# Seven block products in place of eight for three pairs of gate units, and ring buffers in another order

## The chip, the cores and the metric

The kernel runs on one core of a Trainium2 chip. The metric is the time of one execution on the device, in microseconds (us); lower is better. Before the change the median of 3 runs is 960.73 us (960.54 to 960.83). The core's engines are named as the profile names them: PE (TensorE, matrix products), DVE (VectorE), ACT (ScalarE), POOL (GpSimd) and SP (SyncE, which here issues nearly all DMAs).

## The reference, cut to what matters

One encoder layer on 512 tokens of 1024 columns: three token mixers side by side, a gated sum of them, an output projection, a norm, and a mixture of 16 experts of which each picks 64 tokens.

```python
z = jnp.einsum('bsd,df->bsf', x, w_in[l])
q_na, k_na, v_na, q_g, k_g, v_g, q_m, gate_logits = jnp.split(z, _split_points(), axis=-1)
...
branches = jnp.stack([y_na, y_gqa, y_mem], axis=2)                 # 3 mixers, 512 wide each
proj = jnp.einsum('bsgk,gkd->bsgd', branches, w_branch[l])
gates = jax.nn.sigmoid(gate_logits + b_gate[l]).reshape(B, S, N_BRANCH, D)
merged = jnp.sum(gates * proj, axis=2)
mix = jnp.einsum('bsd,de->bse', merged, w_out[l])
x = layer_norm(DN_ALPHA * x + mix, ln1_g[l], ln1_b[l])
ffn = expert_choice_ffn(x, w_router[l], w_gate_up[l], w_down[l])
x = layer_norm(DN_ALPHA * x + ffn, ln2_g[l], ln2_b[l])
```

The change concerns `gate_logits` of the last mixer that is computed, the neighbourhood attention (NA, branch 0): a product of the 512 tokens with a 1024 x 1024 block of `w_in`.

## The kernel before

**Weights as units.** All weights of the mixers, `w_in`, `w_branch` and `w_out`, come as 74 units of 512 KB (`wu`), tiles of 128 partitions x 1024 fp32 values. Class `Stream` brings them in program order: `_dma` has SP load the next unit into one half of the tile `raw_twin`, `_split` makes two tiles of it, a high part (ACT casts to fp32r, L100) and a low part (DVE subtracts the high part from the value, L101). `prefetch` keeps splits ahead of use and up to two loads ahead of the splits.

**A gate unit.** A unit of `w_in` holds 128 output columns for all 8 blocks of 128 inputs. `t_unit` multiplies it with the tokens, which lie transposed and split as `xh` and `xl`: for each of the 8 blocks three matmuls of 128 x 512, high x high, high x low and low x high (L284 to L286), 24 in all, summed in one PSUM buffer. A gate unit ends with a tanh on ACT (L505), which reads PSUM and writes the tile `sg`. The gates of NA are units 54 to 61, eight in a row (`g_na_gates`); then come units 62 to 65 (`w_branch` of NA, products `pr`) and 66 to 73 (`w_out`, products `wo`).

**Order.** The kernel stands under a manual schedule: each engine executes its instructions in program order. `run(gen, every)` drives a generator of PE work and, at each of its yields, steps the attention and takes one item from the list `bg`. While the gates run, `bg` holds three small steps of the router: `router_scale` (four DVE operations), `router_sums` (one small matmul into the PSUM tile `wps`) and `router_centre` (two DVE operations that read `wps`). PSUM has buffers of four tags: `mm` 3, `S` 2, `T` 2, `Y` 1; gates, `pr` and `wps` take `mm` in turn.

**Expert weights.** Behind the units come the experts' weights, 2 MB or 1 MB a block, loaded by SP into homes in SBUF in the order of `RING`; a home is a tile that an earlier stage must have left. `Ring.load` issues a block, and SP waits there until the home is free. The first loads are put behind loads of units by the table `after`: `_dma` calls `after[i]` behind unit i. What else fits comes behind the output projection's units with `ring.upto`, and then a block each time one is used up.

```python
    def gate_piece(g, j, dst):
        u, = ws.take()
        ws.prefetch()
        acc = PB("mm", f"gate{g}{j}")
        t_unit(acc, u, xh, xl)
        return lambda: nc.scalar.activation(dst, acc, AF.Tanh, bias=bg_t[:, g * 8 + j:g * 8 + j + 1], scale=0.5)
```

Of the kernel before, what the change touches and what calls it, by code (L numbers as in the profile page):

```python
# [18 lines left out]
P = 128  # L19
D = 1024  # L20
S = 512
KD = 8
# [50 lines left out]
def layer_kernel(ctx: ExitStack, tc: tile.TileContext, xt, xn, first0, wu, bgate, rpb, gains, wrt,  # L73
                 lnp, lnt, wx, csn, nmask, tri, iota, out, dbg=None):
    nc = tc.nc
# [12 lines left out]
    def R(tag, shape, name, dt=F32, bufs=None):  # L88
        return rp.tile(shape, dt, name=name, tag=tag, bufs=bufs)
# [3 lines left out]
    def PB(tag, name, shape=(P, 512)):  # L93
        return ps.tile(list(shape), F32, name=name, tag=tag, bufs=PS_BUFS[tag])
# [4 lines left out]
    def hi_lo(hi, lo, src):  # L99
        nc.scalar.copy(hi, src)  # L100
        nc.vector.tensor_tensor(lo, src, hi.bitcast(F32), op=ALU.subtract)  # L101
# [40 lines left out]
    def home(i):  # L142
        if NV + 2 <= i < NV + 4:
            if not wide_v:
                wide_v.append(R("Q3", [P, 4, 1024], "whl_v", F32R))
            j = 2 * (i - NV - 2)
            return wide_v[0][:, j], wide_v[0][:, j + 1]
        i = (i - 2 * (i >= NV + 4) - NV) % 3
        return los[:, 3] if i == 2 else R("hi", [P, 1024], f"whi{i}", F32R, bufs=2), los[:, i]


    class Stream:
        AHEAD_DMA = 2

        def __init__(self):
            self.nd = 0
            self.ns = 0
            self.used = 0
            self.raw = {}
            self.hl = {}  # L160

        def _dma(self):
            i = self.nd
            if 2 <= i < 10:
                if i in (2, 6):
# [4 lines left out]
            nc.sync.dma_start(t, wu[i])  # L170
            self.raw[i] = t
            self.nd += 1
            for f in after.pop(i, ()):
                f()
# [28 lines left out]
    after = {}  # L203
    ws = Stream()
# [18 lines left out]
    xh = R("G0", [P, KD, S], "xh", F32R)  # L223
    xl = R("G1", [P, KD, S], "xl", F32R)
# [34 lines left out]
    bg_t = consts[:, 480:504]  # L259
# [74 lines left out]
    ST = {}  # L334
# [50 lines left out]
    bg = []  # L385
# [128 lines left out]
    def g_branch(g, first, pre=None):  # L514
        if first:
            ST["macc"] = R("M", [P, KD, S], "macc")
        macc = ST["macc"]
        for jp in range(4):
            th = []
            for jj in range(2):  # L520
                t = R("t", [P, S], f"th{g}{jp}{jj}", bufs=2)
                th.append(t)
                ev = gate_piece(g, 2 * jp + jj, t)
                yield
                ev()
# [12 lines left out]
            if pre:  # L538
                yield from pre(jp)

    def g_na_qk(hp):
# [4 lines left out]
        for i in range(2):  # L546
# [5 lines left out]
            for h in range(2):  # L552
# [8 lines left out]
                else:  # L561
# [3 lines left out]
                    for o in (hb, lb):  # L565
                        nc.vector.tensor_tensor(klo[o:o + 64, h], src, k[o:o + 64].bitcast(F32), op=ALU.subtract)

    def g_na_gates():
        sg = R("Q4", [P, KD, S], "sg")
        ST["sg"] = sg  # L570
        for j in range(8):
            ev = gate_piece(0, j, sg[:, j])
            yield
            ev()


    def recip_norm(pt, sm, heads):
# [102 lines left out]
    def na_bias(hp):  # L680
        bf = R("bf", [P, 2, 8, 48], f"bf{hp}")
        for bq in range(2):
            for c in range(8):
                p0 = bq * 64 + c
                nc.sync.dma_start(bf[p0:p0 + 57:8], bass.AP(
                    tensor=rpb.tensor, offset=rpb.offset + 2 * hp * 8 * 63 + 15 - 8 * bq - c,
                    ap=[[64 * 63, 8], [63, 16], [1, 48]]))
        if hp % 2 == 0:
            bm = R("Q4", [P, 2, 3, 256], f"bm{hp}")
        else:  # L690
            bm = ST["b01"][:, 2:4].rearrange("p a n -> p (a n)")[:, :1536].rearrange("p (h t n) -> p h t n", h=2, t=3)
        for ty in range(3):
            for h in range(2):
                nc.gpsimd.tensor_tensor(
                    bm[:, h, ty].rearrange("p (b r c) -> p r b c", b=4, r=8),
                    bf[:, h, :, 16 - 8 * ty:48 - 8 * ty].rearrange("p r (b c) -> p r b c", b=4),
                    mask_t[:, ty, None, :].to_broadcast([P, 8, 32]).rearrange("p r (b c) -> p r b c", b=4),
                    op=ALU.add)
        ST[f"bm{hp}"] = bm
# [69 lines left out]
    class Attn:  # L769
# [4 lines left out]
        def add(self, us):  # L774
            self.units += us
# [144 lines left out]
    wsum = wtmp[:, 4][:, :2 * NEXP].rearrange("p (a e) -> p a e", a=2)  # L920
# [75 lines left out]
    def load_x1(h):  # L996
        nc.sync.dma_start(X1[:, 2 * h:2 * h + 2], xn[:, 2 * h:2 * h + 2])
# [1 line left out]
    def x1(m):  # L999
        return X1[:, m]  # L1000

    for i, f in enumerate((lambda: load_x1(0), lambda: load_x1(1), lambda: ring.more(5), load_tri, lambda: ring.more(6))):
        after[N_UNITS - 5 + i] = [f]
    run(g_na_proj())
    top = cp.tile([48, 64], F32, name="top")
# [117 lines left out]
    for kp in range(4):  # L1123
        u, = ws.take()
# [759 lines left out]
```

## Time and profile before

| | us |
|---|---|
| median of 3 runs | 960.73 |
| the profiled execution, its own time | 960.27 |
| its span in the trace | 958.5 |
| PE busy | 942.4 (98%) |
| weight loads of PE (beside matmuls) | 608.5 (63%) |
| DVE busy | 451.1 (47%) |
| ACT busy | 277.3 (29%) |
| POOL busy | 97.4 (10%) |

DMA moves 251.18 MB, a mean of 262 GB/s over the span. "Busy" of PE includes time in which its pipelined matmuls wait for operands that stream in, so 98% doesn't say that PE is the limit everywhere. The page cuts the span into 40 slices of 24 us; one row there shows the rate of DMA in each slice. Slices 0 to 15 are mixers with little DMA, slices 21 to 38 are the experts; the gates of NA fall into slices 15 to 17. A row of a timeline or of a group reads: engine, line, operation, output tile <- input tiles, partitions x elements.

### The profile page before, as it was taken

The numbers are of one execution on the slowest core, as the hardware profiler recorded it, in microseconds if no ns is written. First come the engines' busy times: TensorE is split into PE (matmuls) and PEld (weight loads), VectorE is DVE, ScalarE is ACT, GpSimd is POOL, SyncE is SP. The second block draws the span as 40 slices with busy tenths as digits, with TensorE's granted clock in tenths as the row PEclk, the third lists the DMA queues.
The fourth block names the chain that finished last, engine by engine and source line by source line (L and its number), as shares of the span: only waits on it lengthen the run. The fifth ranks groups of instructions, "written<-read, shape, count | busy, mean of one in ns | idle before, by whom it ended". The sixth has DMA issues, their size and how long they took to land.

```text
span 958.5 us, 12982 instructions
## 1 busy us (share of the span) xinstructions
PE 942.4 (98%) x5262; PEld 608.5 (63%) x5262; DVE 451.1 (47%) x855; ACT 277.3 (29%) x545; POOL 97.4 (10%) x112
## 2 busy tenths in 40 slices
PE   9999999999999999999999999999999999999997
PEld 9899878888888888888886333433334333533345
DVE  6347668764376567237464121653222313231426
ACT  6334453543344454233232111100011000100123
POOL 0102303000122231000023004000000000000004
PEclk9999999999999999999999999999999999999999
DMA  9321211211433322566929999999999999999992
GB/s 363 114 67 67 66 67 44 67 48 64 116 85 110 103 83 66 206 247 262 377 78 381 428 428 424 426 431 430 429 431 430 431 430 431 429 431 429 431 420 111
DMA packets 40807, 251.18 MB, mean 262 GB/s; under 512 B 13198, under 2 KB 13582, under 8 KB 25516
## 3 DMA queue, kind: packets, MB, share of 16 engines
q1 hardware_dynamic: 40604, 250.10, 64.8%
q8 instruction: 41, 0.67, 0.3%
q10 hardware_dynamic: 144, 0.26, 0.1%
q14 instruction: 18, 0.15, 0.0%
HBM read 247.46 MB, written 2.10 MB: 260 GB/s over the span
## 4 chain that ended last, share of the span: by engine, by line
PE 89%; DMA 4%; DVE 4%; POOL 1%; ACT 1%; issue 1%; DVEq 0%; ACTq 0%; POOLq 0%
PE g L1322 11%; PE u L1322 10%; PE y L1358 10%; PE gate L284 4%; PE gate L285 4%; PE gate L286 4%; DMA w<-in_wx 4%; PE pr L284 2%; PE pr L285 2%; PE pr L286 2%; PE gy L672 2%; PE ga L1282 2%; PE cb L1455 2%; PE nqk L284 2%; PE nqk L286 2%; PE nqk L285 2%
## 5 line engine op out<-in xcount | busy, mean ns | idle before, releaser
L1322 PE MATMUL g<-w,xs 128*64 128x512 f32 x508 | 133.9, 606 | 1.9 <-DMA w<-in_wx 1.8
L1322 PE MATMUL u<-w,xs 128*64 128x512 f32 x508 | 130.5, 592 | 0.0
L1358 PE MATMUL y<-w,hT 128*64 128x512 f32 x480 | 106.4, 594 | 2.1 <-DMA w<-in_wx 1.3
L1322 PEld LDWEIGHTS u<-w,xs 128*64 128x64 f32 x508 | 36.5, 137 | 72.5 <-issue 71.7
L101 DVE TENSOR_TENSOR los<-raw_twin,whi 128x1024 fp32r<-128x1024 f32 x42 | 53.5, 1275 | 57.5 <-ACT whi L100 57.3
L101 DVE TENSOR_TENSOR y<-y,y 64x512 fp32r<-64x512 f32 x28 | 19.3, 689 | 128.1 <-ACT y L100 128.1
L100 ACT CAST y<-y 64x512 fp32r<-64x512 f32 x28 | 16.2, 580 | 215.6 <-PE y L1358 205.1
L1358 PEld LDWEIGHTS y<-w,hT 128*64 128x64 f32 x480 | 34.0, 137 | 70.1 <-issue 65.2
L286 PE MATMUL gate<-xh,los 128*128 128x512 f32 x192 | 74.8, 390 | 0.0
L1322 PEld LDWEIGHTS g<-w,xs 128*64 128x64 f32 x508 | 30.5, 136 | 52.1 <-issue 44.5
L284 PE MATMUL gate<-xh,whi 128*128 128x512 f32 x144 | 57.2, 397 | 0.0
L285 PE MATMUL gate<-xl,whi 128*128 128x512 f32 x144 | 56.1, 390 | 0.0
L1458 DVE TENSOR_TENSOR acc<-acc,cb 128x512 f32<-128x512 f32 x56 | 35.6, 683 | 37.9 <-PE cb L1456 37.9
L100 ACT CAST whi<-raw_twin 128x1024 fp32r<-128x1024 f32 x42 | 44.1, 1050 | 9.6 <-PE wo L1120 6.5
L1538 POOL TENSOR_TENSOR acc<-acc,ln2g 128x512 f32<-128x512 f32 x8 | 10.0, 1274 | 353.5 <-ACT y L100 353.1
L286 PEld LDWEIGHTS gate<-xh,los 128*128 128x128 f32 x192 | 36.0, 188 | 7.7
L648 ACT ACTIVATE att_twin<-gs,nm 128x512 f32<-128x512 f32 x32 | 21.7, 684 | 49.9 <-DVE nm L647 49.9
L1332 ACT ACTIVATE tg<-g 128x512 f32<-128x512 f32 x16 | 9.5, 597 | 88.8 <-PE g L1322 88.8
L101 DVE TENSOR_TENSOR los<-raw_twin,los 128x1024 fp32r<-128x1024 f32 x20 | 25.0, 1248 | 19.6 <-ACT los L100 19.5
L284 PEld LDWEIGHTS gate<-xh,whi 128*128 128x128 f32 x144 | 27.0, 188 | 6.5 <-issue 1.2
L1345 DVE COPY hT<-ht 128x512 f32<-128x512 f32 x15 | 10.4, 691 | 43.5 <-PE ht L1340 43.4
L285 PEld LDWEIGHTS gate<-xl,whi 128*128 128x128 f32 x144 | 27.1, 188 | 5.3
(461 smaller groups left out, 1883.1 us busy)
## 6 DMA issues: line engine op xcount, KB each, us to landing
w<-in_wx SPq DMA_DIRECT2D x74, 2048.0 KB
w<-in_wx SPq DMA_DIRECT2D x43, 1024.0 KB
raw_twin<-in_wu SPq DMA_DIRECT2D x65, 512.0 KB
raw<-in_wu SPq DMA_DIRECT2D x8, 512.0 KB
xr<-in_xt SPq DMA_DIRECT2D x4, 512.0 KB
macc<-in_xn SPq DMA_DIRECT2D x2, 1024.0 KB
out<-acc SPq DMA_DIRECT2D x7, 256.0 KB
first<-in_first SPq DMA_DIRECT2D x4, 384.0 KB
```

The costliest lines, as they stand in the source:

```text
L100: nc.scalar.copy(hi, src)
L101: nc.vector.tensor_tensor(lo, src, hi.bitcast(F32), op=ALU.subtract)
L284: nc.tensor.matmul(acc, w_h, rh[:, k], start=(k == 0), stop=False)
L285: nc.tensor.matmul(acc, w_h, rl[:, k], start=False, stop=False)
L286: nc.tensor.matmul(acc, w_l, rh[:, k], start=False, stop=(k == nk - 1))
L648: nc.scalar.activation(self.p[:, h], self.s[h], AF.Exp, bias=nm[:, h:h + 1], accum_out=self.sm[:, h:h + 1])
L672: nc.tensor.matmul(self.y[h * 64:h * 64 + 64, :P], ST["vg"][:, kc, kvh * 64:kvh * 64 + 64], self.pt[:, h, kc], start=(kc == 0), stop=(kc = ...
L1282: nc.tensor.matmul(g, XH[:, m, c], oh[:, m, sl], start=(m == 0), stop=False)
L1322: nc.tensor.matmul(GU[e][b][hf * 64:hf * 64 + 64], xs, w[b][hf] if isinstance(w[b], list) else w[b][:, hf * 512:hf * 512 + 512], start=(k ...
L1358: nc.tensor.matmul(y[o * 64:o * 64 + 64], hT[:, c, hf * 64:hf * 64 + 64], w[j][:, o * 512:(o + 1) * 512], start=(k == 0 and j == 0), stop= ...
L1455: nc.tensor.matmul(cb, g[:, m], yh[:, c], start=True, stop=False)
L1458: nc.vector.tensor_tensor(a, a, cb, op=ALU.add)
```

## The change

Units 54 and 55 run as before. Units 56 to 61 go in three pairs. A pair is a product of two by two blocks: two units (128 columns each) by two halves of the 1024 inputs on the weights' side, two halves of the inputs by two halves of the tokens (256) on the other. In place of eight block products it computes seven, on sums of blocks, in the Winograd form of Strassen's scheme:

- **Token sums** (`token_sums`), once for all pairs: four sums t1 to t4 of quarter blocks of the tokens, each 128 x 1024, by eight DVE additions and subtractions and four splits (ACT cast, DVE subtraction). Twelve steps of it are put into `bg` ahead of branch 1, the last two splits at the start of the gates. They lie in the tiles of tag Q6 (t1, t2) and Q2 (t3, t4).
- **Weight sums** (`GatePair.sums`), for each pair: four POOL operations of 128 x 512 on two SBUF tiles, and then two splits of 1024 (ACT and DVE). Of the pair's first unit all is split, of its second one half.
- **Products**: seven of 12 matmuls of 128 x 256 (`block_product`), each into half of a PSUM buffer of tag mm, S or T.
- **Sums of products**: per pair a copy on ACT and seven additions on DVE that read PSUM (L660), then tanh on ACT on `sg` in SBUF.

Units 58 to 61 are loaded in one go into the tile of tag Q7, which the attention used until then. `sg` now shares a Q4 tile (`bmsg`) with the attention's bias, and half of that tile takes the first pair's weight sums and, ahead of that, the token sums' working values. The ring's homes come in another order, and the first five blocks are put behind the loads of units 64 to 68 in place of 60, 62, 64 and 66.

```diff
-RING = (("Q2", 2), ("Q1", 2), ("Q5", 2), ("Q7", 2), ("Q4", 2), ("Q3", 2), ("Q6", 2), ("raw", 1), ("Q9", 2), ("VS", 1),
+G0 = 54
+RING = (("Q7", 2), ("Q5", 2), ("Q6", 2), ("Q1", 2), ("Q2", 2), ("Q3", 2), ("Q4", 2), ("raw", 1), ("Q9", 2), ("VS", 1),
...
+            elif G0 + 4 <= i < G0 + 8:
+                if i == G0 + 4:
+                    self.wide = R("Q7", [P, 4, 1024], f"raw{i}")
+                t = self.wide[:, i - G0 - 4]
...
+        def room(tag, ns):
+            t = R(tag, [P, 4, 1024], f"t{ns[0]}", F32R).rearrange("p n (k c) -> p n k c", k=4)
...
+        steps = [first, op(s0, s0, l(0, 1), ALU.add), op(s0, s0, l(0, 0), ALU.subtract),
+                 op(s1, h(1, 1), s0, ALU.subtract), lambda: split(1, s0), op(s1, s1, l(1, 1), ALU.add),
+                 op(s0, h(1, 0), s1, ALU.subtract), lambda: split(2, s1), op(s0, s0, l(1, 0), ALU.add),
+                 op(s1, h(1, 1), h(0, 1), ALU.subtract), op(s1, s1, l(1, 1), ALU.add), op(s1, s1, l(0, 1), ALU.subtract)]
+
+        def rest():
+            room("Q2", (3, 4))
+            split(3, s1)
+            split(4, s0)
...
+        def sums(self):
+            t = R(self.tag, [P, 4, 1024], f"wsum{self.i}", F32R)
+            self.s = t[:, 0:2], t[:, 2:4]
+            self.sums_raw = ST["q4"][:, 2:4] if self.i == G0 + 2 else R("VS", [P, 2, 1024], f"wsr{self.i}")
+            q = [self.sums_raw[:, n // 2, (n % 2) * 512:(n % 2) * 512 + 512] for n in range(4)]
+            (a11, a12), (a21, a22) = ((r[:, :512], r[:, 512:]) for r in self.raw)
+            g = nc.gpsimd.tensor_tensor
+            g(q[0], a21, a22, op=ALU.add)
+            g(q[1], q[0], a11, op=ALU.subtract)
+            g(q[2], a11, a21, op=ALU.subtract)
+            g(q[3], a12, q[1], op=ALU.subtract)
...
+    def block_product(acc, w, t):
+        wh, wl = (x.rearrange("p (k c) -> p k c", k=4) for x in w)
+        for k in range(4):
+            nc.tensor.matmul(acc, wh[:, k], t[0][:, k], start=(k == 0), stop=False)
+            nc.tensor.matmul(acc, wh[:, k], t[1][:, k], start=False, stop=False)
+            nc.tensor.matmul(acc, wl[:, k], t[0][:, k], start=False, stop=(k == 3))
+
+    def gate_pair(w, j, sg, nxt):
+        B = {(k, t): (x_block(xh, k, t), x_block(xl, k, t)) for k in range(2) for t in range(2)}
+        p = {n: PB(t, f"gp{n}{j}")[:, :256] for n, t in zip((1, 6, 5, 2, 7, 3, 4), ("mm", "S", "mm", "T", "S", "T", "mm"))}
...
+        nxt[0]()
+        block_product(p[1], w.half(w.a1, 0), B[0, 0])
+        nc.scalar.copy(u[:, 0], p[1])
+        block_product(p[6], w.s_part(1), TB[2])
+        add(u[:, 1], u[:, 0], p[6])
+        nxt[1]()
+        block_product(p[5], w.s_part(0), TB[1])
+        add(v[:, 0], u[:, 1], p[5])
+        block_product(p[2], w.half(w.a1, 1), B[1, 0])
+        add(sg[:, j, lo], u[:, 0], p[2])
+        block_product(p[7], w.s_part(2), TB[3])
+        add(sg[:, j + 1, hi], v[:, 0], p[7])
+        add(v[:, 1], u[:, 1], p[7])
+        nxt[2]()
+        yield
+        block_product(p[3], w.s_part(3), B[1, 1])
+        add(sg[:, j, hi], v[:, 0], p[3])
+        tanh(j)
+        nxt[3]()
+        block_product(p[4], w.half(w.a2, 1), TB[4])
+        add(sg[:, j + 1, lo], v[:, 1], p[4])
+        tanh(j + 1)
+        nxt[4]()
+        yield
...
-        for j in range(8):
-            ev = gate_piece(0, j, sg[:, j])
+        rest()
+        w = GatePair(G0 + 2, "Q1")
+        for j in range(2):
...
+        for j in (2, 4, 6):
+            ws.used += 2
+            if j < 6:
+                n = GatePair(G0 + j + 2, "Q5" if j == 2 else "Q1")
+                nxt = (n.sums, n.first, lambda: n.split(0), lambda: n.split(1), n.second)
+            else:
+                no = lambda: None
+                nxt = (no, lambda: ws.prefetch(1), no, no, lambda: ws.prefetch(2))
+            yield from gate_pair(w, j, sg, nxt)
...
-    for i in range(4):
-        after[N_UNITS - 14 + 2 * i] = [lambda: ring.more(4)]
+    for i in range(5):
+        after[G0 + 10 + i] = [lambda: ring.more(5)]
...
+    token_steps, rest = token_sums()
+    bg.extend(token_steps)
     run(g_branch(1, False, between), 0.5)
...
-    bg.extend([lambda: None, router_scale, lambda: None, router_sums, router_centre])
+    bg.extend([lambda: None, lambda: None, router_scale, lambda: None, router_sums, router_centre])
```

The order of instructions on DVE where the gates run, in the kernel before: subtractions that split the units to come (names starting with `whi` or `los` are their homes), and the router's last two steps.

```order
L101 TENSOR_TENSOR los<-raw_twin,los 128x1024
L101 TENSOR_TENSOR los<-raw_twin,whi_3513 128x1024
L101 TENSOR_TENSOR los<-raw_twin,whi_3545 128x1024
L938 COPY lnT<-wps 128x16
L939 SCALAR_TENSOR_TENSOR wr_t<-wps,wr_t 128x128
L101 TENSOR_TENSOR los<-raw_twin,los 128x1024
```

The same engine after the change, from the second pair's first additions to the router's `wps`. `gu` and `gv` are partial sums of products, `gp` the products in PSUM, `wsum` the split weight sums of the third pair, `wsr` those sums before the split.

```order
L102 TENSOR_TENSOR los<-raw_3503,whi_3629 128x512
L660 TENSOR_TENSOR gu_3639<-gu_3639,gp_3633 128x256
L102 TENSOR_TENSOR los<-raw_3503,whi_3673 128x1024
L660 TENSOR_TENSOR gv_3640<-gu_3639,gp_3634 128x256
L660 TENSOR_TENSOR bmsg<-gu_3639,gp_3635 128x256
L660 TENSOR_TENSOR bmsg<-gv_3640,gp_3636 128x256
L660 TENSOR_TENSOR gv_3640<-gu_3639,gp_3636 128x256
L102 TENSOR_TENSOR wsum_3641<-wsr_3642,wsum_3641 128x1024
L660 TENSOR_TENSOR bmsg<-gv_3640,gp_3637 128x256
L102 TENSOR_TENSOR wsum_3641<-wsr_3642,wsum_3641 128x1024
L660 TENSOR_TENSOR bmsg<-gv_3640,gp_3638 128x256
L102 TENSOR_TENSOR los<-raw_3503,los 128x512
```

The additions that clear the second pair's products stand between, and behind, subtractions that wait for casts and for POOL's sums; the last addition (of `gp_3638`, the second pair's seventh product) stands behind two subtractions of 1024.

POOL after the change, from the last sum of branch 1 on (`macc`). `raw_3503` is the Q7 tile of units 58 to 61, `wsr_3520` takes the second pair's weight sums.

```order
L542 TENSOR_TENSOR macc<-macc,tm_3389 128x512
L1066 MEMSET wtmp 128x128
L1072 MEMSET ones_h 128x128
L623 TENSOR_TENSOR bmsg<-raw_twin 128x512
L624 TENSOR_TENSOR bmsg<-bmsg,raw_twin 128x512
L625 TENSOR_TENSOR bmsg<-raw_twin 128x512
L626 TENSOR_TENSOR bmsg<-raw_twin,bmsg 128x512
L623 TENSOR_TENSOR wsr_3520<-raw_3503 128x512
L624 TENSOR_TENSOR wsr_3520<-wsr_3520,raw_3503 128x512
L625 TENSOR_TENSOR wsr_3520<-raw_3503 128x512
```

The rows from L623 on are new; before, memsets for the router's sums followed the two of L1066 and L1072 directly, far later.

PE after the change, the border between the second and third pair: `gp44` is the second pair's seventh product, `gp16` the third pair's first, on tile `whi1_3673`.

```order
L652 MATMUL gp44_3638<-t3_3397,los_69 128x256
L650 MATMUL gp16_3754<-xh_73,whi1_3673 128x256 [waits DVE_49,Activation_49]
L651 MATMUL gp16_3754<-xl_74,whi1_3673 128x256
L652 MATMUL gp16_3754<-xh_73,los_69 128x256
```

A gate unit before had 24 rows of 128x512 at this place; the first matmul of each product now stands behind the operands' split and behind whatever clears its PSUM buffer.

More of the change, by code (lines that the diff above doesn't have):

```diff
@@ new lines, in layer_kernel, with __init__, first, split @@
+    class GatePair:
+        def __init__(self, i, tag):
+            self.i, self.tag = i, tag
+            self.raw = [ws.raw[i], ws.raw[i + 1]]
+        def sums(self):
[9 more added lines that the diff above has]
+            g(q[3], a12, q[1], op=ALU.subtract)
+        def first(self):
+            ws._split()
+            self.a1 = ws.hl.pop(self.i)
+        def split(self, n):
+            hi_lo(self.s[0][:, n], self.s[1][:, n], self.sums_raw[:, n])
+        def second(self):
+            raw = ws.raw.pop(self.i + 1)
+            self.a2 = home(self.i + 1)
+            hi_lo(self.a2[0][:, 512:], self.a2[1][:, 512:], raw[:, 512:])
+            ws.ns += 1
+        def s_part(self, n):
+            return tuple(x[:, n // 2, (n % 2) * 512:(n % 2) * 512 + 512] for x in self.s)
+        def half(self, u, h):
+            return tuple(x[:, h * 512:h * 512 + 512] for x in u)
@@ L568, in g_na_gates @@
     def g_na_gates():
-        sg = R("Q4", [P, KD, S], "sg")
+        sg = ST["q4"].rearrange("p a (b s) -> p (a b) s", s=S)
         ST["sg"] = sg
-        for j in range(8):
-            ev = gate_piece(0, j, sg[:, j])
-            yield
-            ev()
+        rest()
+        w = GatePair(G0 + 2, "Q1")
+        for j in range(2):
+            u, = ws.take()
+            if j == 0:
+                w.first()
+                w.sums()
+            else:
+                w.split(0)
+            acc = PB("mm", f"gate0{j}")
+            t_unit(acc, u, xh, xl)
+            yield
+            nc.scalar.activation(sg[:, j], acc, AF.Tanh, bias=bg_t[:, j:j + 1], scale=0.5)
@@ new lines, in g_na_gates @@
+        w.split(1)
+        w.second()
+        for _ in range(6):
+            ws._dma()
+        for j in (2, 4, 6):
[3 more added lines that the diff above has]
+                nxt = (n.sums, n.first, lambda: n.split(0), lambda: n.split(1), n.second)
+            else:
+                no = lambda: None
+                nxt = (no, lambda: ws.prefetch(1), no, no, lambda: ws.prefetch(2))
+            yield from gate_pair(w, j, sg, nxt)
+            w = n
@@ L688, in na_bias @@
         if hp % 2 == 0:
[L689 removed]
+            if hp == 0:
+                ST["q4"] = R("Q4", [P, 4, 1024], "bmsg")
+            bm = ST["q4"][:, 0:2].rearrange("p a n -> p (a n)")[:, :1536].rearrange("p (h t n) -> p h t n", h=2, t=3)
         else:
@@ L1000, in x1 @@
         return X1[:, m]
-    for i, f in enumerate((lambda: load_x1(0), lambda: load_x1(1), lambda: ring.more(5), load_tri, lambda: ring.more(6))):
+    for i, f in enumerate((lambda: load_x1(0), lambda: load_x1(1), lambda: ring.more(6), load_tri, lambda: ring.more(7))):
         after[N_UNITS - 5 + i] = [f]
```

23 lines of the change are left out of this document (added).

## The prediction

> **What bounds the kernel now.** I read the slices first, then stretches, then the chain and SP's waits.
>
> ```profile
> span 958.5 us, 12982 instructions
> ...
> GB/s 363 114 67 67 66 67 44 67 48 64 116 85 110 103 83 66 206 247 262 377 78 381 428 428 424 426 431 430 429 431 430 431 430 431 429 431 429 431 420 111
> ```
> ```profile
> 390.40:423.50 33.10, 33.10 (x149) 27.40 (x148) 9.12 (x13) 10.03 (x13) 0.00 (x0) 1.00 0.70 274
> ...
> 484.00:500.00 16.00, 16.00 (x110) 14.59 (x110) 11.00 (x48) 6.22 (x14) 3.68 (x14) 1.00 0.00 1
> ...
> 514.00:944.00 430.00, 425.62 (x2243) 170.29 (x2242) 136.46 (x257) 52.08 (x98) 14.67 (x12) 1.00 0.99 418
> ```
>
> The three rows are stretches: length, then busy time (and count) of PE, weight loads, DVE, ACT and POOL, the clock, the DMA share and GB/s. From 390.4 to 423.5 the last six of the eight gate units run: PE is busy in all 33.1 us, DVE in 9.1, POOL not at all. From 514 to 944 the experts' weights stream at 418 GB/s with the DMA engines 99% busy, so there DMA is the bound although PE is also called busy. Between lies a hole: from 484 to 500 nothing moves. SP's rows say why.
>
> ```profile
> 475.67 0.40 SPq L834 DMA_DIRECT2D wxa<-in_wx  x1
> 500.34 0.33 SPq L843 DMA_DIRECT2D w<-in_wx  x1
> ```
> ```profile
> SPq L843 <- PE woc L1119: 24.2, 1, 24.2
> ```
> ```profile
> 875.53 38.19 DMA w<-in_wx
> ```
>
> SP issues the last of the early expert blocks at 475.7 and then waits 24.2 us for PE to finish the output projection (woc), whose weights occupy the next ring home. Only then does the stream resume, and the chain at the end still runs through it: a block issued at 875.5 lands 38 us later. So a microsecond that PE gains or loses between the gates and 500.3 moves the resumption, and with it the whole weight stream and the end, by one microsecond, as long as the early blocks have landed by then. They have some 16 us to spare (484 to 500).
>
> **The change part by part.** First PE. Rows of a timeline: start, duration, engine, line, operation, tiles.
>
> ```profile
> 418.02 0.39 PE L284 MATMUL gate<-xh,los 128*128 128x512 f32 x1
> ...
> 423.24 0.39 PE L286 MATMUL gate<-xh,los 128*128 128x512 f32 x1
> ```
> ```profile
> 69.78 0.28 PE L306 MATMUL gq<-whi,xh 128*128 128x256 f32 x1
> ...
> 71.10 0.28 PE L308 MATMUL gq<-whi,xl 128*128 128x256 f32 x1
> ```
>
> The first two are the first and last of a gate unit's 24 matmuls: (423.24 - 418.02) / 23 = 0.227 us from one to the next, 5.45 us a unit. The other two are the first and last of 12 matmuls on 256 columns, split the same way as the new products: 1.32 / 11 = 0.120 us. Three pairs go from 144 matmuls of 512 columns, 144 x 0.227 = 32.6 us, to 3 x 7 x 12 = 252 of 256 columns, 252 x 0.120 = 30.2 us. **Gain 2.4 us**, if PE never waits. The seven products save one eighth of the columns; a 256-column matmul costs 0.007 us more than half a 512-column one, and that takes back 1.7 us of the 4.1.
>
> The Trainium skill, "TensorE: Matmul & The Clock Gate", section Back-to-back issue gap, has two rules for this. An isolated stream costs N / 2.4 + 2.5 ns, 109 and 216 ns here, and by it the gain would be 31.1 - 27.5 = 3.6 us (an estimate). Its figures for sustained pairs of weight load and matmul, 81 ns at 128 columns and 131 at 512, speak against the change: a straight line gives 98 ns at 256, and 24.6 us in place of 18.9, a loss. The rows here, 0.120 and 0.227, lie near the first rule and far from the second.
>
> The new work is on the other engines. Before, a gate unit needs one cast on ACT and one subtraction on DVE; DVE then sat 4.2 us:
>
> ```profile
> 419.88 1.23 DVE L101 TENSOR_TENSOR los<-raw_twin,whi 128x1024 fp32r<-128x1024 f32 x1 [4.21 <-ACT whi L100]
> ```
> ```profile
> 418.22 0.69 ACT L505 ACTIVATE sg<-gate,consts 128x512 f32<-128x512 f32 x1 [3.81 <-PE gate L286]
> 418.81 1.04 ACT L100 CAST whi<-raw_twin 128x1024 fp32r<-128x1024 f32 x1
> ```
> ```profile
> 390.94 0.42 DVE L101 TENSOR_TENSOR yn<-ny,yn 128x256 fp32r<-128x256 f32 x1 [3.94 <-ACT yn L100]
> 391.29 0.28 DVE L930 TENSOR_TENSOR wtmp<-wr_t,lnT 128x128 f32<-128x128 f32 x1
> ...
> 392.22 0.38 DVE L931 TENSOR_REDUCE wtmp<-wr_t 128x16 f32<-128x128 f32 x1
> ```
>
> A pair now needs on DVE three subtractions of 1024 (1.23), one of 512 (about 0.65, half), and seven adds from PSUM, priced as the 0.42 row; about 7.3 us of 10.1. ACT has three casts (1.04), half a cast, two tanh (0.69), a copy (0.37): 5.5 us. POOL has four sums of 128x512. Each engine fits; what doesn't fit easily is the alternation between them. The next rows show POOL and DVE beside each other.
>
> ```profile
> 263.61 1.74 POOL L694 TENSOR_TENSOR bm<-bf,consts 128x256 f32<-128x256 f32 x1
> ```
> ```profile
> 264.69 1.75 DVE L101 TENSOR_TENSOR los<-raw_twin,whi 128x1024 fp32r<-128x1024 f32 x1
> ```
> ```profile
> 112.96 1.31 POOL L418 TENSOR_TENSOR ropesq<-mkvzs,consts 128x512 f32<-128x512 f32 x1
> 114.24 2.29 POOL L417 TENSOR_TENSOR ropevg<-mkvzs,consts 128x512 f32<-128x512 f32 x1
> ```
> ```profile
> 113.49 1.86 DVE L101 TENSOR_TENSOR los<-raw_twin,whi 128x1024 fp32r<-128x1024 f32 x1 [1.66 <-ACT whi L100]
> ```
>
> A POOL op on two SBUF operands of 128x512 takes 1.31 us alone. The DVE subtraction that starts inside it, at 113.49, takes 1.86 in place of 1.23 and ends 1.08 us after the POOL op does; the next POOL op then takes 2.29. Each waits for the whole of the other, in turn: about 1.15 us of exclusive use for each.
>
> The new chain, step by step. The last attention product ends on PE at about 390.5, and frees Q7, so that SP can issue the loads of units 58 to 61.
>
> ```profile
> 389.88 0.61 PE L761 MATMUL ny<-att_twin,ropevg 128*64 128x128 f32 x8
> ```
> ```profile
> 341.37 0.33 SPq L170 DMA_DIRECT2D raw_twin<-in_wu  x1
> ```
> ```profile
> 344.00:345.00 1.00, 1.00 (x6) 0.84 (x5) 0.97 (x3) 0.78 (x5) 0.00 (x0) 1.00 0.44 92
> ```
>
> A unit's load issued at 341.37 is in by about 344.4, 3.0 us; the next, 512 KB at 420 GB/s, 1.25 us behind it. So unit 59, which POOL's first sum needs, is in at 394.75. First sum, then DVE's subtraction of unit 58, then the second sum, at 1.15 each: 398.2. Cast 399.3; DVE's subtraction waits for the third sum: 400.55; fourth sum 401.7, and the router's four DVE ops behind it (1.2 in the rows above): 402.85. Add of the sixth product 403.2, tanh and cast in ACT's order 404.85, subtraction 406.1, **add of the seventh product 406.4**. PE had finished that product at 390.4 + 10.1 = 400.5, and meanwhile ran the second pair, whose operands are in time by 0.5 to 1.5 us.
>
> For the third pair: tanh, half cast; the half subtraction waits for a sum: 409.2; subtraction of unit 60, behind another sum, 411.4; four adds 412.7; subtraction of the first sums 413.9; add 414.25; tanh and cast 415.9; subtraction 417.15; **add of the second pair's seventh product 417.5**. PE reaches the third pair at 410.85. Its first product needs the PSUM buffer that the first of the four adds clears, 411.8: 0.95 us. Its second needs the low half at 413.95: 0.45. Its third takes the buffer of the second pair's seventh product, because the router's small tile (wps) still holds the next one: 417.55 in place of 415.15, 2.4. Sum **3.8 us of waits**. Two steps in this chain are near ties over who comes first, the router's ops (0.9) and the half subtraction (1.2); both won, 1.7 of waits is left. The order in which they ask says lost; I take off a fifth of the 2.1 and use 3.4.
>
> The twelve token ops on DVE in the stage before hide in DVE's idle time there (it waits 3 to 5 us on ACT or PE between units, as in the rows above), and the four casts go the same way; uncovered they would cost PE at most the 1.2 us of the one that stands ahead of a softmax. I take 0. The loads of expert blocks now begin near 419, not 394, and are some 23 MB up to the output projection's end: 55 us at 430 GB/s, done by about 481. That uses none of the wait that ends at 500. The ring's order permutes seven homes of equal size: 0.
>
> Sum against the profiled execution (960.27 us, its span 958.5 and 1.8 around it; the median of the runs is 960.73): -2.4 + 3.4 = +1.0, so 961.3 for it and **961.7** as a median.
>
> **The rivals.** *Waits half as long* (ties won): waits of 0.5 to 2.4, net -1.9 to 0, 958.8 to 960.7. For it: each tie is 0.3 us or less; against: two DVE subtractions in a row were split by a waiting POOL op at 263 to 265. *No waits*: -2.4, 958.3; for it, with no blocking at all the add of the second pair's seventh product comes at 413.7, when PE wants it. Against: three sums fall inside subtractions in my chain. *Slower*: the first sum of the second pair starts late. Its place is unit 59's landing; the price is one for one, since everything behind hangs on that chain; it decides from 0.9 us later than 394.75 on (net +1.9). For it: the four loads follow each other and no row shows four in one go; 3 us late would be 964.7. *The products don't pay*: if weight loads showed between the shorter matmuls, the new code would lose from 32.6 / 252 = 0.129 us a matmul on; at 0.145 it runs 36.5 us, 3.9 longer than before, with no waits since PE comes later: 964.6. Against: the twelve rows at 0.120, with as many weight loads. (The pair rule of that page would make it some 966.)
>
> **How the numbers follow.** Forecast (waits 2.4 to 4.3, 960.7 to 962.6): 0.50. Half as long 0.20. No waits, below 958.8: 0.06. Slower, above 962.65: 0.23. Products that don't pay: 0.01. A measurement can tell about 0.2%, 1.9 us: faster 0.06, same 0.70, slower 0.24. The range 959.0 to 964.7 leaves out the no-wait case and the slower ones beyond 3 us late.
>
> **What would show it.** In the changed profile: 12 matmuls of a product 1.44 us apart; PE's first waits of this stage before the third pair's first and third product, ended by DVE adds; DVE subtractions of 1.8 and POOL sums of 2.3 between 394 and 417; the wps buffer as cause; SP's long wait still on woc, its end moved by PE's net, and nothing moving just before it. Waits in the stage before, or early blocks still landing when woc ends, would make me wrong.

## The result

The changed kernel takes 969.65 us, median of 6 runs (966.27 to 972.30), beside 960.64 us (959.95 to 961.65) for the kernel before: a ratio of 1.0098, 95% interval 1.0082 to 1.0114. It is slower, by 9 us where 1 us was forecast, and outside the range. The profiled execution took 971.23 us. Its page answers to the rows of before so (the last two rows are the granted clock and the rate of DMA in 40 slices):

```profile
span 969.1 us, 13275 instructions
...
PEclk9999999999999999999899999999999999999999
...
GB/s 359 112 66 66 66 66 49 61 73 38 118 97 96 98 82 66 131 163 423 329 87 338 416 426 418 426 430 431 429 431 428 431 433 430 430 430 431 429 421 112
```

The experts' weights stream at the same 430 GB/s as before, only later. The stretches of the changed kernel, in the columns of the prediction's:

```profile
390.70:427.60 36.90, 33.21 (x257) 32.23 (x255) 24.76 (x39) 14.74 (x21) 16.04 (x14) 0.95 0.33 125
...
500.00:510.00 10.00, 10.00 (x76) 9.40 (x76) 7.12 (x31) 5.33 (x13) 3.53 (x14) 1.00 0.00 0
524.00:954.00 430.00, 425.31 (x2242) 170.00 (x2241) 136.40 (x256) 52.03 (x98) 14.02 (x12) 1.00 0.99 418
```

The first is the three pairs: 36.9 us in place of 33.0, PE busy in 33.2 of them, the granted clock 0.95 in place of 1.00. The stretch from 500 to 510 is part of the hole without DMA, which now reaches from 492.5 to 510.6 (before: 483.5 to 500.3). SP's waits and timeline say that the stream still hangs on the output projection, which now ends 10.3 us later (510.65 in place of 500.34):

```profile
SPq L988 <- PE woc L1266: 24.0, 1, 24.0
```
```profile
510.65 2.27 SPq L988 DMA_DIRECT2D w<-in_wx  x3
```

So the loss lies ahead of that point, and PE's waits between 389 and 512 (instruction <- what ended the wait: us in all, times, longest) tell where; first the wait of the kernel before at this addition, then those of the changed kernel:

```profile
PE x1t L1024 <- DVE macc L1041: 0.3, 1, 0.3
```
```profile
PE x1t L1171 <- DVE macc L1188: 4.0, 1, 4.0
PE gp L650 <- DVE bmsg L660: 2.2, 1, 2.2
PE gp L650 <- DVE gv L660: 1.2, 1, 1.2
PE gp L652 <- DVE wsum L102: 0.2, 1, 0.2
```

Two of the three waits of `gp` are ones that were forecast: 1.2 us ahead of the third pair's first product and 2.2 us ahead of its third. The third, 0.2 us at 407.1, stands in the second pair and was not; together they are 3.6 us. The longest, 4.0 us, was not forecast either: it stands near the end of the first half of the output projection (`wo`), at 468.6. The wait is put down to a DVE addition, which stood behind the split of a unit. The chain of waits says what that split waited for:

```profile
439.19 9.32 DMA raw_twin<-in_wu
...
450.95 9.75 DMA raw_twin<-in_wu
...
463.14 6.44 DMA raw_twin<-in_wu
```

Two units take 9.3 and 9.8 us from issue to landing, where PE needs one every 5.5 us. Between 425 and 475 us ACT's casts, the first step of a split, wait 17.5 us in all for the loads of units, in seven waits; in the kernel before they don't wait for one there. Between 424 and 462 us the loads of before and of after (two pieces of the DMA view, before first) are these:

```profile
DMA packets 1494, 9.57 MB, mean 252 GB/s; under 512 B 162, under 2 KB 162, under 8 KB 988
...
w<-in_wx SPq DMA_DIRECT2D x2, 2048.0 KB
```
```profile
DMA packets 1759, 14.82 MB, mean 390 GB/s; under 512 B 189, under 2 KB 189, under 8 KB 993
...
w<-in_wx SPq DMA_DIRECT2D x4, 2048.0 KB
```

Four expert blocks of 2 MB in place of two are issued there. And the granted clock fell twice, where it is 1.00 in the same stretches of the kernel before. Stretches of 1 us behind the wait of 2.2 us, and of 2 us around the one of 4.0 us (the clock is the third figure from the end):

```profile
419.00:420.00 1.00, 1.00 (x8) 1.00 (x9) 0.00 (x0) 1.00 (x3) 0.00 (x0) 0.86 0.00 0
420.00:421.00 1.00, 1.00 (x7) 1.00 (x6) 0.90 (x4) 1.00 (x3) 0.00 (x0) 0.50 0.00 0
...
422.00:423.00 1.00, 1.00 (x6) 1.00 (x6) 0.87 (x2) 0.00 (x0) 0.00 (x0) 0.50 0.00 0
423.00:424.00 1.00, 1.00 (x10) 1.00 (x9) 0.42 (x1) 0.00 (x0) 0.00 (x0) 0.93 0.44 90
```
```profile
470.00:472.00 2.00, 0.00 (x0) 0.00 (x0) 1.24 (x2) 0.73 (x1) 0.00 (x0) 0.73 0.90 375
472.00:474.00 2.00, 1.36 (x6) 1.27 (x7) 1.93 (x4) 0.21 (x1) 0.00 (x0) 0.50 0.97 280
474.00:476.00 2.00, 2.00 (x6) 1.52 (x5) 0.63 (x1) 0.38 (x1) 0.00 (x0) 0.50 1.13 458
476.00:478.00 2.00, 2.00 (x12) 1.89 (x10) 1.38 (x2) 0.58 (x1) 0.00 (x0) 0.56 0.98 420
```

Of the 10.3 us, then, 0.3 stand ahead of the pairs, 3.9 in the pairs and 6.1 in `wo` (31.5 us from its first matmul to that of `woc`, 25.3 before): 3.7 of more waiting, and 2.4 that fit the 5 us that PE then runs at half clock.

### The profile page after: what moved, and what is told of

It reads as the page before. It is cut to its first block, busy times and chain, and to the rows that moved or that the text cites. A ratio compares the mean times of both kernels' runs of the same rounds, so it can differ in the third digit from the quotient of the medians.

```text
span 969.1 us, 13275 instructions
## 1 busy us (share of the span) xinstructions
PE 945.3 (98%) x5370; PEld 615.8 (64%) x5370; DVE 484.1 (50%) x896; ACT 286.4 (30%) x558; POOL 125.7 (13%) x124
## 4 chain that ended last, share of the span: by engine, by line
PE 83%; DMA 7%; DVE 5%; ACT 2%; POOL 2%; issue 1%; DVEq 0%; ACTq 0%; POOLq 0%
PE g L1469 11%; PE u L1469 10%; PE y L1505 10%; DMA w<-in_wx 4%; PE gate L289 3%; PE gate L291 3%; PE gate L290 3%; DMA raw_twin<-in_wu 3%; PE pr L289 2%; PE pr L290 2%; PE pr L291 2%; PE gy L815 2%; PE ga L1429 2%; PE cb L1602 2%; PE nqk L291 2%; PE nqk L289 1%
## 5 line engine op out<-in xcount | busy, mean ns | idle before, releaser
L102 DVE TENSOR_TENSOR los<-raw_twin,whi 128x1024 fp32r<-128x1024 f32 (+1 forms) x40 | 50.9, 1272 | 43.8 <-ACT whi L101 43.7
L1469 PEld LDWEIGHTS g<-w,xs 128*64 128x64 f32 x508 | 30.4, 136 | 52.2 <-issue 44.5
L291 PE MATMUL gate<-xh,los 128*128 128x512 f32 x144 | 56.1, 390 | 0.0
L101 ACT CAST whi<-raw_twin 128x1024 fp32r<-128x1024 f32 (+1 forms) x40 | 41.6, 1040 | 14.8 <-DMA raw_twin<-in_wu 13.2
L289 PE MATMUL gate<-xh,whi 128*128 128x512 f32 x112 | 44.6, 398 | 0.0
L290 PE MATMUL gate<-xl,whi 128*128 128x512 f32 x112 | 43.7, 390 | 0.0
L291 PEld LDWEIGHTS gate<-xh,los 128*128 128x128 f32 x144 | 27.0, 188 | 5.8
L102 DVE TENSOR_TENSOR los<-raw_twin,los 128x1024 fp32r<-128x1024 f32 x18 | 22.5, 1251 | 15.1 <-ACT los L101 15.0
L542 POOL TENSOR_TENSOR macc<-macc,tm 128x512 f32<-128x512 f32 x8 | 18.5, 2311 | 80.0 <-DVE tm L541 80.0
L873 ACT ACTIVATE att_twin<-att_twin,nm 128x256 f32<-128x256 f32 x32 | 16.1, 503 | 38.2 <-DVE nm L871 38.2
```

What stands on the lines that cost most here:

```text
L289: nc.tensor.matmul(acc, w_h, rh[:, k], start=(k == 0), stop=False)
L290: nc.tensor.matmul(acc, w_h, rl[:, k], start=False, stop=False)
L291: nc.tensor.matmul(acc, w_l, rh[:, k], start=False, stop=(k == nk - 1))
L1469: nc.tensor.matmul(GU[e][b][hf * 64:hf * 64 + 64], xs, w[b][hf] if isinstance(w[b], list) else w[b][:, hf * 512:hf * 512 + 512], start=(k ...
```

## The experiments

Two theories were set against rivals. **A:** the 6.1 us in `wo` come from the places of the loads. **B:** the 3.9 us in the gates come from PSUM buffers and DVE's chain. The table has medians and, from the start times in PE's and SP's timelines, the length of the gates (from the first matmul of the last six units to the first `pr`), of `wo`, and the time at which SP resumes the stream.

| kernel | median us | gates | wo | resumes at |
|---|---|---|---|---|
| before | 960.64 | 33.0 | 25.3 | 500.3 |
| after | 969.65 | 36.9 | 31.5 | 510.7 |
| e1_thin | 965.21 | 37.3 | 25.3 | 504.9 |
| e2_wps | 966.49 | 33.4 | 28.9 | 504.7 |
| e3_both | 961.40 | 33.1 | 25.3 | 501.0 |
| e4_spare | 963.50 | 35.5 | 25.3 | 502.4 |
| e5_nopool | 958.05 | 30.6 | 25.3 | 498.2 |
| e6_early | 961.59 | 34.6 | 25.3 | 502.3 |
| e7_early_router | 958.68 | 30.9 | 25.3 | 498.8 |
| e8_before_packed | 965.50 | 33.0 | 30.4 | 505.1 |
| e9_router | 958.69 | 31.2 | 25.3 | 498.3 |
| e10_oldring | 959.19 | 30.9 | 26.3 | 498.9 |
| e11_router_mm | 961.40 | 33.7 | 25.3 | 500.7 |
| e12_packed | 963.26 | 31.0 | 30.2 | 502.8 |

**Fewer blocks behind the units.**

```diff
-    for i in range(5):
-        after[G0 + 10 + i] = [lambda: ring.more(5)]
+    for i in range(3):
+        after[G0 + 10 + 2 * i] = [lambda: ring.more(5)]
```

> The changed kernel with three of the five expert blocks that stand behind units 64 to 68 left there (behind 64, 66 and 68), the other two later, where room for them is found behind the output projection's units; the gates untouched. Theory A: in the changed kernel 7 blocks and 2 MB of other loads share 49 us with the output projection's units (20.9 MB, all that 425 GB/s brings), each unit takes 9 to 10 us to land, and PE's wait of 4.0 us at 468.6 with the half clock behind it (together 6.1 of the 10.3 us lost) comes from that: about 963.5 us, units landing in 5 us or less, no wait over 1 us in the output projection. Rival: units are late because the gates delay their splits, whatever is loaded beside them: 969 as before.

Measured: 965.21 us (964.22 to 965.55), 4.4 less than the change. `wo` is back at 25.3 us, and PE's wait ahead of `x1t` is as in the kernel before:

```profile
PE x1t L1171 <- DVE macc L1188: 0.3, 1, 0.3
```

ACT's casts wait 0.3 us for loads of units in place of 17.5. Theory A holds. The expected 963.5 took the 6.1 us, read from the change's profiled execution, off its median, and that execution is 1.6 us above the median; profiled against profiled the gain is 6.3 us.

**The router's tile in another PSUM buffer.**

```diff
-        wps.append(PB("mm", "wps")[:, :2 * NEXP])
+        wps.append(PB("Y", "wps")[:, :2 * NEXP])
```

> The changed kernel with the router's small PSUM tile (wps) in the buffer of tag Y in place of one of tag mm, nothing else. Theory B: the wps tile shifts the turn of the mm buffers, so that the third pair's first and third product wait for additions of the second pair (1.2 and 2.2 us), and the second wait brings the half clock from 419.7 to 423.1: both waits go, waits for split operands of about 2 us take their place, and the gates end about 4 us earlier (near 423.5 in the trace). The total gains less, 0 to 4 us (966 to 969), since loads, not PE, set the output projection. Rival: the additions themselves are late because DVE and POOL exclude each other, and PE then waits for operands as long as it waited for buffers: gates end near 427.5, total 969 to 970.

Measured: 966.49 us. The gates took 33.4 us, 3.5 less, no wait for a buffer is left and the clock stays at 1.00 there. Theory B holds for the gates. In `wo` PE still waits, 2.9 us, but the clock stays at 1.00 behind that wait in this profile, and `wo` takes 28.9 us in place of 31.5. The median is 3.2 lower, within the 0 to 4 that were expected.

**Both edits.**

> Both edits: three blocks in place of five behind units 64 to 68, and wps in the buffer Y. If both theories hold the losses add up and both go: 959.5 us, within 0.2% of the kernel before (gain 2.4 of products, about 2 us of operand waits left, no half clock). If only the loads matter, 963.5; if only the buffers, 966.

Measured: 961.40 us, ratio to the kernel before 1.0010 (1.0001 to 1.0020): 8.2 of the 9 us are gone, 1.9 us less than was expected (959.5). What is left of waits in the pairs is for split operands:

```profile
PE gp L652 <- DVE wsum L102: 1.0, 2, 0.8
PE gp L652 <- DVE los L102: 0.6, 1, 0.6
```

**A spare product in the idle time**, on top of the first edit.

```diff
         nxt[1]()
+        if j == 6:
+            block_product(PB("Y", "spare6")[:, :256], w.s_part(1), TB[2])
         block_product(p[5], w.s_part(0), TB[1])
```

> The thinner loads as in the first kernel, and one more block product of 12 matmuls, whose result is not used, ahead of the third pair's third product, where PE sat idle for 2.2 us. If the half clock behind that wait comes from PE's being idle, the clock stays at 1.00 between 416 and 424, and though PE does 1.4 us more of work the gates end 1.7 us earlier than with thinner loads alone: 961.8 beside 963.5. Rival: the half clock comes from something else (load, phase), then it stays and the time is the same or up to 1.4 us longer.

Measured: 963.50 us beside 965.21, 1.7 less with more work done, and the gates 35.5 us beside 37.3. Stretches of 2 us, first of the kernel with the spare product, then of the one without it:

```profile
418.00:420.00 2.00, 1.85 (x15) 1.85 (x16) 0.70 (x2) 1.87 (x4) 0.00 (x0) 1.00 0.00 0
420.00:422.00 2.00, 2.00 (x19) 2.00 (x19) 2.00 (x6) 0.59 (x1) 0.00 (x0) 1.00 0.00 0
```
```profile
418.00:420.00 2.00, 0.83 (x4) 0.84 (x5) 1.11 (x2) 0.85 (x2) 0.00 (x0) 0.82 0.00 0
420.00:422.00 2.00, 2.00 (x11) 2.00 (x11) 1.59 (x5) 1.59 (x3) 0.00 (x0) 0.50 0.00 0
```

19 matmuls in 2 us in place of 11: the half clock came from PE's being idle, and it costs 1.7 us beyond the wait.

**No weight sums on POOL**, on top of both edits.

```diff
-            g(q[0], a21, a22, op=ALU.add)
-            g(q[1], q[0], a11, op=ALU.subtract)
-            g(q[2], a11, a21, op=ALU.subtract)
-            g(q[3], a12, q[1], op=ALU.subtract)
...
-            hi_lo(self.s[0][:, n], self.s[1][:, n], self.sums_raw[:, n])
+            hi_lo(self.s[0][:, n], self.s[1][:, n], self.raw[n])
```

> The kernel with both edits (fewer blocks behind units 64 to 68, wps in Y), and no weight sums: POOL's twelve additions are left out and the splits read the loaded units in their place, so six of eight gate units come out wrong. Theory: DVE subtractions and POOL additions run in turn, and the time that DVE loses so (the rows of 1.67 to 2.25 us in place of 0.7 to 1.23) is what leaves PE's waits for split operands, 2.8 us in the kernel with both edits: without POOL's work under 0.8 us of waits is left and the time is 2 us lower, 959.4 beside 961.4. Rival: the waits come from the order of ACT's and DVE's own queues (router, tanh, casts), then they stay and so does the time, 961.4.

This kernel leaves out the twelve additions, and the splits read the loaded units in place of the sums. Measured: 958.05 us, and 30.55 us for the 252 matmuls of the gates, 0.121 us each: PE doesn't wait there at all. So without POOL's work the waits do go; whether by the time of the sums themselves or by their clash with DVE, this run can't tell. The next runs show that it is not the only thing whose removal does that.

**Earlier weight sums; and the router's scaling earlier, with them and alone.** First the sums of the third pair into free tiles, then the list `bg` as well, then the list without the sums:

```diff
...
+            q4s = {G0 + 2: lambda: (q4[:, 2], q4[:, 3]), G0 + 4: lambda: (ST["wsr"][:, 0], ST["wsr"][:, 1]),
+                   G0 + 6: lambda: (q4[:, 3], ST["wsr"][:, 0])}
...
```
```diff
-    bg.extend([lambda: None, lambda: None, router_scale, lambda: None, router_sums, router_centre])
+    bg.extend([router_scale, lambda: None, lambda: None, lambda: None, router_sums, router_centre])
```

> Both edits, and the third pair's weight sums in tiles that are free earlier (a quarter of the Q4 tile and half of the second pair's VS tile), so that POOL adds them right behind the second pair's sums, near 403 to 408, in place of 407.3 to 413.9, with all the work done. If the third pair's waits (0.7 and 0.9 us) come from POOL's additions lying across DVE's splits at 408.8 and 410.8, they go, and the time falls by 1.5 us, to 959.9. Rival: they now lie across the router's operations and the splits at 406, and delay the second pair as much: 961.4.

> As the kernel with early sums, and the router's four scaling operations on DVE behind the first gate in place of in the midst of the second pair's chain. If these 2.3 us of DVE time ahead of the first addition of the chain that leads over tanh and cast to the second pair's last split set PE's wait at 407, that wait (0.4 us) goes too: 959.4 to 959.9, 0.1% faster than the kernel before, hardly more than can be measured. Rival: no change against early sums alone.

> Both edits and the router's four scaling operations behind the first gate, without the earlier weight sums. The kernel with earlier sums alone gave nothing (961.6 beside 961.4), the one with both gave 958.7. If the router's place is the whole cause: 958.7 to 959.2 here. If the two are needed together (the sums still lie across the splits at 408 and 411 and PE waits 0.7 and 0.9 us there): 960 to 960.5.

Measured: 961.59, 958.68 (ratio 0.9977, 0.9968 to 0.9986) and 958.69 us (0.9985, 0.9976 to 0.9994). The sums' place gives nothing, as the rival of the first said; the router's place gives 2.7 us alone. DVE's rows of the kernel with early sums and late router show both (start, duration):

```profile
401.87 1.38 DVE L1082 TENSOR_TENSOR wtmp<-wr_t,lnT 128x128 f32<-128x128 f32 x1
403.28 0.39 DVE L1083 TENSOR_REDUCE wtmp<-wtmp 128x16 f32<-128x128 f32 x1
403.59 0.96 DVE L1082 TENSOR_TENSOR wr_t<-wr_t,lnT 128x128 f32<-128x128 f32 x1
404.58 0.38 DVE L1083 TENSOR_REDUCE wtmp<-wr_t 128x16 f32<-128x128 f32 x1
404.89 0.40 DVE L665 TENSOR_TENSOR bmsg<-gv,gp 128x256 f32<-128x256 f32 x1
407.02 2.32 DVE L102 TENSOR_TENSOR wsum<-wsr,wsum 128x1024 fp32r<-128x1024 f32 x1 [1.73 <-ACT wsum L101]
```

The addition at 404.89 starts the chain tanh, cast, split; ahead of it stand 3.0 us of the router's operations, the first of which takes 1.38 us beside a POOL sum and 0.28 us in the kernel before. And the moved sums only moved the clash: the split at 407.02 now takes 2.32 us in place of 1.23. With the router moved, PE's only wait in the pairs of the last kernel is

```profile
PE gp L652 <- DVE wsum L102: 0.4, 1, 0.4
```

although all twelve sums are still there. Taking 2 to 3 us out of that chain at either place is enough; what is taken out beyond that is slack.

**The new places of the loads in the kernel before.**

```diff
-    for i in range(4):
-        after[N_UNITS - 14 + 2 * i] = [lambda: ring.more(4)]
+    for i in range(5):
+        after[N_UNITS - 10 + i] = [lambda: ring.more(5)]
...
-    for i, f in enumerate((lambda: load_x1(0), lambda: load_x1(1), lambda: ring.more(5), load_tri, lambda: ring.more(6))):
+    for i, f in enumerate((lambda: load_x1(0), lambda: load_x1(1), lambda: ring.more(6), load_tri, lambda: ring.more(7))):
```

> The kernel before with the changed kernel's places for the loads alone: five blocks behind units 64 to 68 in place of four behind 60, 62, 64 and 66, and two more behind 71 and 73; its gates and its ring order as they were. Theory A: the same 21 MB must come between the load of unit 64 (416) and that of unit 73 (464), more than 425 GB/s bring in 48 us: units come late and PE waits 1 to 4 us near 464, with the half clock behind it where the wait is long: 962 to 966. Rival: without the gates' delay the units keep up: 960.4.

Measured: 965.50 us (961.77 to 969.21), ratio 1.0044 (1.0026 to 1.0062). PE waits 3.8 us at 464 and the half clock follows, with the old gates:

```profile
467.90 0.66 PE L1024 MATMUL x1t<-ident,macc 128*128 128x128 f32 x4 [3.78 <-DVE macc L1041]
...
469.51 0.63 PE L1118 MATMUL wo<-whi,mh 128*128 128x512 f32 x1
```

(0.63 us is that matmul at half clock; 0.39 at full.) Four pairs of kernels differ in the places of the loads alone (this one and the kernel before; the change and e1_thin; e2_wps and e3_both; e12_packed and e9_router): in the medians the loads cost 4.4 to 5.1 us, whatever the gates do. The eight runs here form two groups that differ in the mean granted clock, which is on record for every run: three of 961.8 to 962.4 us have 0.998 or 0.999, five of 965.2 to 969.2 have 0.993 to 0.996. So here the runs that keep their clock lose 1 to 2 us, and the others 5 to 9. In e2_wps and e12_packed the runs at 0.998 still lose 4.2 to 4.6: the loads cost time without the half clock too.

**The old order of the ring** in the kernel with early sums and router.

> The fastest kernel so far (fewer blocks behind the units, wps in Y, early sums, early router) with the ring's homes in the order of the kernel before. The prediction took the order at nothing. If the first home then is one that the gates still read (Q2, with t3 and t4, read to the last product of the third pair), SP waits for it with the loads of the output projection's units queued behind: the first block is issued some 2 to 4 us later and the time is the same to 2 us longer (958.7 to 960.7), since the units have 2 to 3 us to spare. Rival: no difference, 958.7.

Measured: 959.19 us (ratio 0.9988, 0.9979 to 0.9998), beside 958.68 with the new order (0.9977, 0.9968 to 0.9986). The intervals overlap; `wo` took 1 us longer in the one profile. Nothing that can be told apart.

**The router's tile back in mm; and the packed loads with the best gates**, both with the router's scaling early.

> The changed kernel with fewer blocks behind the units and the router's scaling early, but wps back in a buffer of tag mm: it tells what the buffer alone costs once the chain of additions is 2.4 us earlier. From the rows of the kernel with wps in Y the second pair's last addition ends near 416.4, and PE would want that buffer at 415: if the buffer is a cause of its own, PE waits some 0.5 us ahead of the third pair's first product and 1.5 us ahead of its third, 960.5 us (961.5 if a half clock follows). Rival: with the chain early the buffer no longer matters, 958.7.

> wps in Y and the router's scaling early, with the five blocks behind units 64 to 68 as in the change: the gates at their best, the loads as changed. If the loads cost by themselves, as in the kernel before with the same places for the loads (965.5), PE waits 3 to 5 us near 464, often with a half clock behind it: 963 to 966, about 5 us over the kernel with fewer blocks (958.7). Rival: the units were late because the gates held up their splits: under 960.

Measured: 961.40 and 963.26 us. In the first, PE waits for the buffer again:

```profile
PE gp L650 <- DVE bmsg L660: 2.2, 1, 2.2
```

2.7 us over the kernel with the tile in Y: the buffer is a cause of its own. Its 11 runs form two groups (seven up to 961.50, four from 963.49 on); the profiled one is of the upper group, and yet it resumes the stream at 500.7, so what sets it apart lies behind that point. Its page shows one slice of 24 us there, from 577 to 601, in which the experts' weights came at 388 GB/s where the kernel with both edits has 425, which is 2 us of stream; why stays open. In the second PE waits 3.1 us ahead of `x1t`, 4.6 us over the kernel with fewer blocks: the loads again, with the gates at their best.

## Why the prediction was wrong

**What sets the end** was right: the stream resumes when `woc` ends, and what PE loses before that is lost at the end. The profiled execution is 10.96 us longer, the resumption 10.3 later; in the kernel with early sums and router the resumption is 1.6 earlier and the median 1.9 lower.

**The products** were right: 252 matmuls take 30.55 us without waits, 0.121 us each where 0.120 was forecast, and 2.5 us less than the 33.0 of before. (Two sums of the prediction are off by a tenth, 144 x 0.227 is 32.7 and ACT's operations add up to 5.4 us; neither changes the forecast.)

**The token sums** were right at nothing. They are ten additions and subtractions on DVE, not eight, and four splits; the pairs begin 0.3 us later than before, and in the eleven other profiles of kernels with pairs they begin between 389.9 and 391.0, before and behind the 390.4 of the kernel before.

**The chain on DVE** came about a microsecond late. The additions that were to end at 406.4 and 417.5 ended at 407.5 and 418.8. Waits of 0.95, 0.45 and 2.4 us in the third pair were 1.2, 0.3 (a gap between matmuls, not in the list of waits) and 2.2. That they came out so near is in part luck: PE, too, reached the third pair a microsecond later than assumed, at 411.8. The buffer that `wps` takes out of turn was the cause. The near tie over the router's operations was lost, as the order in which they ask said: they took 2.3 us on DVE where 1.2 was put down, and moving them gave 2.7, more than the 0.9 of the tie.

**What a wait costs** was mis-sized. The term "waits, 3.4" counted idle time. The gates took 36.9 us where the products alone take 30.2: 3.6 idle, 1.5 from 17 matmuls at up to 0.22 us in place of 0.12 (the half clock), and 1.6 in single gaps of 0.1 to 0.3 us, most of them right before and behind the waits. So 6.6 in place of 3.4.

**The loads** are the step that failed, and cost the most: 6.1 us. The prediction moved the early blocks to 419, summed them to 23 MB, found them landed by 481 and concluded that this "uses none of the wait that ends at 500". 419 and its 55 us make 474, not 481, but the time given was nearly right: 22.2 MB moved from 423 to 481.5, and then SP issued the last 2.1 MB at 485, once the last unit had been split, and these landed by 492.5. The hole is there from then on, 18 us long. But only the end of the blocks was looked at, not what runs beside them: the units of the output projection go through the same DMA engines behind the blocks that stand ahead of them in SP's queue. Six blocks, 2 MB of `xn` and ten units, 19.9 MB, were put into the 49 us between the loads of units 64 and 73; that is 403 GB/s, of the 430 at which the experts' weights stream. Before it was three blocks, 13.6 MB in 48 us. (The expectation ahead of the first run counts a seventh block; SP issues it behind unit 73.) So the units landed late, although there was room for two of those blocks behind the last unit, where the first run put them. That the blocks' homes are taken by the new operands until 420 is part of the change; that all of them stand in front of units is not needed. The two first runs separate the two losses, the third adds them up, and the kernel before with the new places shows the second alone.

The rival "slower" asked for a late unit 59. It was 1.0 us late (POOL's first sum starts at 395.73, not 394.75), just beyond the 0.9 that the rival asked for, and the chain 1.1 to 1.3. But the idle time in the pairs stayed at 3.6 us, so that is not what made the time.

## What to carry to other kernels

When loads are moved later, compare bytes with time in every stretch in which something urgent shares the DMA engines, not only at the end of the last load; here a small load that was needed next took 9 to 10 us behind large ones issued ahead of it, and 3.0 us earlier in the kernel with little else to load. An idle gap of PE of 2 us may cost a good deal more than its length, here 1.7 us more. Small operations of another job that stand in the midst of a chain across engines are worth moving before the chain's own work is: here four router operations decided 2.7 us.

## What the runs showed of the hardware

The granted clock fell to a half behind idle times of 2.2 us (from 419.7 to 423.1, 3.4 us) and 4.0 us (from 470.9 to 477.7, 6.8 us; the borders are worked out from the clock of stretches of 1 and 2 us), and not behind one of 1.2 us. The length of the idle time alone does not decide it. In the profile of e6_early 1.9 us were enough (0.50 from 409.2 to 412.7, 3.4 us); in that of e2_wps PE was idle for 2.9 us at 466, in that of e11_router_mm for 2.2 us at 414, and the clock stayed at 1.00. The Trainium skill, "TensorE: Matmul & The Clock Gate", section What's actually happening, puts this down to windows of about 3.4 us that run freely, of which an idle one halves the clock. The lengths measured, about one and two such windows, agree, and so does it that idle times of one length fall out differently from one profile to the next; idle times of 1.9 and 2.2 us, well under a window, were enough here.

The clock goes with the spread of the changed kernel's runs. In order of time they are 966.27 us (mean granted clock 0.998, as in the profile of before), 967.81 (0.995), 968.07 (0.996), 971.23 (0.993), 972.24 and 972.30 (0.991 both). From the first to the last the clock loses 0.007 of 966 us, 6.8 us, and the time grows by 6.0. So the change costs 5.6 us in the run that keeps the clock, and the other 3.4 us of the median's 9 come with the half clock.
